# A hybrid encoder layer on one core: weight loads moved to another queue, diagonal copies moved to the VectorE, and the 32x32 products of an inverse spread over four array tiles

## The chip, the core and the metric

The kernel runs on one core of a Trainium2 chip. The engines are written as in the profile: PE is the matrix engine (TensorE), PEld its weight loads, DVE the VectorE, ACT the ScalarE, POOL the GpSimd, SP the SyncE, which here only issues DMAs. The metric is the device time of one execution in microseconds (us); lower is better.

## The reference, cut to what matters

One encoder layer on 1024 tokens of width 1024, float32. One input projection feeds three branches: windowed attention, a bidirectional RWKV-7 scan, and sigmoid gates. The branches are lifted, gated, summed and projected; two more residual blocks (a feed-forward one and a small gated one) follow.

```python
def rwkv7_bidir_scan(r, w, k, v, a, b):
    def step(state, inp):
        r_t, w_t, k_t, v_t, a_t, b_t = inp
        sa = jnp.einsum('dbhij,dbhj->dbhi', state, a_t)
        state = (state * w_t[..., None, :] + sa[..., :, None] * b_t[..., None, :]
                 + v_t[..., :, None] * k_t[..., None, :])
        y = jnp.einsum('dbhij,dbhj->dbhi', state, r_t)
        return state, y
...
        h = rms_norm(x, norm_mix[i])
        proj = h @ w_in[i]
        attn = windowed_gqa(q, k, v, sink[i])
        rw = rwkv7_time_mix(zr, w0[i], w2[i], a0[i], a2[i], g2[i], k_k[i], k_a[i],
                            r_k[i], lnx_w[i], lnx_b[i])
        gates = jax.nn.sigmoid(proj[..., O_GATE:].reshape(bsz, s, N_BRANCH, D_MODEL))
        merged = gates[..., 0, :] * (attn @ w_up_attn[i]) + gates[..., 1, :] * (rw @ w_up_rwkv[i])
        x = x + merged @ w_out[i]
        hf = rms_norm(x, norm_ffn[i])
        x = x + jnp.square(jax.nn.relu(hf @ w_ff1[i])) @ w_ff2[i]
        hp = rms_norm(x, norm_ple[i])
        x = x + (p[i] @ w_ple[i]) * jax.nn.sigmoid(hp @ w_ple_gate[i])
```

The kernel computes the scan in 16 chunks of 64 tokens. Each chunk needs, for each of 8 heads and 2 directions, the inverse of a 64x64 triangular matrix; it is built from two 32x32 inverses on its diagonal and one product of three 32x32 matrices off it.

## The kernel before, in words

Dense products are made with three matmuls each: an operand is split into a high and a low part (`split`: a copy on ACT, then a subtraction on DVE or POOL), and `mm3_steps` yields after each of high x high, low x high, high x low. A group of such matmuls is a "step" of a filler, and the fillers are what keeps PE busy while the scan and the attention wait for other engines.

In order of time:

- 0 to about 280 us: normalisation, projections of the RWKV columns in four pairs of heads, with decay and in-context rates. For each pair, `vt` is eight transposes of z (`vtp`, L633), copied by ACT and stored to `v_d` (L635); `bv` (L636 to L640) is a bonus term that uses PE sums `px` (L619, L620) and is stored to `bv_d`. Both `vt` and `bv` take the buffer with tag "vt", which has one copy.
- 280 to about 480 us: the attention, in 8 blocks of 128 queries (loop over `n`, from L914): scores `sc` (L934), softmax on DVE and ACT, transposes `pt` (L955), products `po` (L963), a store `at_d`. Steps of `gates(0)` (matmuls `gmm`; weights by `load_w`, staged in `wst` L215, loaded on SP's queue, split into `whi`, `wlo`) stand between them. Inside this loop the triangular matrices of scan block 0 are made too: `low_products` (matmuls `lps` L813 from `la`, `lb`, copied to `lt` L815, four chunk pairs), then `inverse` (copies `Lc`, transpose `Lp`, a recurrence of 31 steps `tmp`/`Z` on DVE, transposes `Zn`, `Zt`).
- 480 to about 770 us: the scan, in four blocks of four chunks. At the start of each block, `inverse_off` makes the 32x32 products: 64 products `qps<-Zn,lt`, copies `Q` (L861), steps of the filler (`between()`, 8 of them), 64 products `qps<-Zt,Q` and `qps<-Q,Zt`, and copies into `zi`. Each product is one matmul in the code and two records in the trace, so a group shows as 128. The inverse of the next block is prepared meanwhile: `low` (one chunk pair of `lps`, ACT's copies `lt` and `Lc` L1279), and `inverse_steps` (the recurrence, from `Lp` L1285). The filler is `beside()`: the rest of the gates, then the lift of the attention branch (`uaps`, from weights `wuhi`/`wulo`, the attention output `aTh`/`aTl`, and a gate read back from `g_d`).
- 770 to about 800 us: `epilogue(1)`, group normalisation of the scan's second half: sums `mups`, logarithms `lv` and exponentials `ysq` on ACT.
- 800 us to the end: the lift of the scan branch (`mmc`, gated in `g1t`, split into `mh`/`ml`), the output projection `mmo` with weights `wo0h`/`wo0l`, the feed-forward part (`ff1ps`, `ff2ps`) and the last gate.

Each engine runs its instructions in a fixed order that a scheduler makes from the code, with priorities; `after(a, b)` puts instruction a behind b in it. PE's array can be used in tiles of 32 rows by 32 columns; a matmul whose operands lie on partitions 32r to 32r+31 and whose output lies on partitions 32c to 32c+31 uses row group r and column group c.

Of the kernel before, what the change touches and what calls it, by code (L numbers as in the profile page):

```python
# [17 lines left out]
P = 128  # L18
# [19 lines left out]
EXPIN = (1, 0)  # L38
# [17 lines left out]
GATT = 1  # L56

# [10 lines left out]
LOW_AT = 3  # L68
# [77 lines left out]
def block_kernel(ctx: ExitStack, tc: tile.TileContext, I: dict, out: bass.AP):  # L146
# [49 lines left out]
    def split(hi, lo, src, lo_eng=None, pin=False):  # L196

        a = nc.scalar.copy(hi, src)  # L198
        b = (lo_eng or nc.vector).tensor_tensor(out=lo, in0=src, in1=hi.bitcast(F32), op=ALU.subtract)  # L199
        if lo_eng is nc.gpsimd:  # L200
            on_pool[0] = b
        if pin:
            tc.keep_in_program_order(a)
            tc.keep_in_program_order(b)

    def load_w(pl, tag, src, n, bufs=2, sbufs=2, lo_eng=None, stag=None, parts=1, stages=()):
# [5 lines left out]
        for i in range(0, k, step):  # L212
            spl, stg, sb = stages[(i // step) % len(stages)] if stages else (pl, stag or tag + "_st", sbufs)
            st = spl.tile([P, step, n], F32, name="wst", tag=stg, bufs=sb)
            nc.sync.dma_start(st, src[:, i:i + step])  # L215
# [105 lines left out]
    def gates(h, ms=range(2 * KT), mm=nc.tensor.matmul, lo_of=lambda m: nc.gpsimd):  # L321

        for m in ms:
            c0 = O_GATE + m * P
            hi, lo = load_w(PW, "w", w_col(c0), P, parts=2, lo_eng=lo_of(m))
# [191 lines left out]
    with ExitStack() as s1:  # L517
# [106 lines left out]
        def add_bonus(p, rk, vz):  # L624
# [11 lines left out]
            bv = A1.tile([P, T], F32, name="bv", tag="vt", bufs=1)  # L636
# [213 lines left out]
    def inverse_off(pl, ps_of, lt, zz, zi, mm, between):  # L850
# [5 lines left out]
        for i in range(32):  # L856
            for r in (0, 2):
                mm(qss[i // 16][g[r + 1], i % 16, :], lt[g[r], i, 32:64], Zn[g[r], i, :], start=True, stop=True)
        for hp, qs in enumerate(qss):
            for r in (1, 3):  # L860
                nc.scalar.copy(Q[g[r], 16 * hp:16 * hp + 16, :], qs[g[r]])  # L861
# [7 lines left out]
        for i in range(32):  # L869
            mm(qss[i // 16][g[0], i % 16, :], Q[g[1], i, :], Zt[g[1], i, :], start=True, stop=True)  # L870
            mm(qss[i // 16][g[3], i % 16, :], Zt[g[3], i, :], Q[g[3], i, :], start=True, stop=True)
        for hp, qs in enumerate(qss):
            nc.scalar.copy(zi[g[0], 16 * hp:16 * hp + 16, 32:64], qs[g[0]])
            nc.scalar.copy(zi[g[3], 16 * hp:16 * hp + 16, 0:32], qs[g[3]])
# [26 lines left out]
    with ExitStack() as s2:  # L901
# [16 lines left out]
        for n in range(NT):  # L918
# [53 lines left out]
            if n == LOW_AT:  # L972
                lts[0] = list(low0)[-1]
# [18 lines left out]
    def beside():  # L992
# [18 lines left out]

        def weights(m, st=None):
            hi = UA.tile([P, NP, P], F32R, name="wuhi", tag="wu_hi", bufs=3)
            lo = UA.tile([P, NP, P], F32R, name="wulo", tag="wu_lo", bufs=3)
            split(hi, lo, st or load_wu(UA, m))
# [12 lines left out]
        for h in range(2):  # L1028
            hs = slice(512 * h, 512 * h + 512)
            for m in range(KT):  # L1030
                hi, lo = ahead.pop(0)
                if (h, m) != (0, 0) and (h, m) < (1, KT - 1):
                    ahead.append(weights((m + 1) % KT))
                g = UA.tile([P, 512], F32, name="gta", tag="g1t", bufs=2)
                nc.sync.dma_start(g, g_d[m, :, hs])
# [27 lines left out]
    def epilogue(e):  # L1063
# [50 lines left out]
        for p in range(NP):  # L1114
# [12 lines left out]
            split(rwh[:, p, :], rwl[:, p, :], rs.rearrange("q a t -> q (a t)"))  # L1127
# [873 lines left out]
```

## Time and profile before

| what | value |
|---|---|
| three runs, median | 1685.11 us (1683.96, 1685.11, 1685.51) |
| profiled execution | 1685.89 us |
| its span, first to last instruction | 1684.1 us |
| around the span | 1.79 us |
| PE busy | 1615.9 us, 96% |
| PEld / DVE / ACT / POOL busy | 1307.8 / 1134.6 / 844.5 / 103.1 us |
| mean granted TensorE clock | 0.986 |
| DMA | 269.23 MB, mean 160 GB/s |

PE is busy for 96% of the span, so the time is PE's work plus the 68.2 us in which PE has nothing to run, plus what PE loses where its granted clock is below 1. The clock is granted in stretches; a slower stretch shows in the windows of the profile as a mean below 1. A row of the view of waits names the engine that waited, the line and tile it waited to start, and what ended the wait.

### The profile page before, as it was taken

The page shows a single profiled execution, that of the slowest core. Times are in us where ns is not written, and L with a number is a line of the kernel's source. Part 1 is how long each engine was busy: PE and PEld are TensorE (multiplying, and loading weights), DVE is VectorE, ACT ScalarE, POOL GpSimd, SP SyncE. Part 2 cuts the span into 40 slices and gives each one's busy share as a digit, 9 for nine tenths or more (in the row PEclk, how much of TensorE's full clock was granted, in tenths as well). Part 3 has the DMA queues.
Part 4 walks back from the last instruction along what each step waited for, and adds up shares of the span by engine and source line. Part 5 has one row for each costly group of instructions (what it writes and reads, how often), then busy time and mean ns, then how long its engine had stood idle before and what let it go on. Part 6 is the DMA issues. An engine that isn't in the chain of part 4 may idle for free.

```text
span 1684.1 us, 31165 instructions
## 1 busy us (share of the span) xinstructions
PE 1615.9 (96%) x12280; PEld 1307.8 (78%) x12280; DVE 1134.6 (67%) x2055; ACT 844.5 (50%) x1535; POOL 103.1 (6%) x113
## 2 busy tenths in 40 slices
PE   7999998899999999898999999999999999999998
PEld 7987776776677787676778788888888888888887
DVE  5648998265947596777744876667667877685342
ACT  5557887367744545456313554444435344544121
POOL 3440000221200000000000000000000000000000
PEclk9999999999999999799999999999999999999999
DMA  6353556764286554547652154444449865564110
GB/s 223 82 155 98 171 163 202 227 172 130 88 230 198 139 179 134 163 130 238 207 179 100 57 177 161 144 165 147 138 167 349 273 204 162 164 212 148 38 41 38
DMA packets 200834, 269.23 MB, mean 160 GB/s; under 512 B 47728, under 2 KB 103920, under 8 KB 200688
## 3 DMA queue, kind: packets, MB, share of 16 engines
q1 hardware_dynamic: 190752, 254.14, 47.6%
q0 software_dynamic: 9792, 12.59, 2.9%
q8 instruction: 96, 1.57, 0.4%
q10 hardware_dynamic: 144, 0.52, 0.1%
q14 instruction: 50, 0.41, 0.1%
HBM read 186.45 MB, written 80.74 MB: 159 GB/s over the span
## 4 chain that ended last, share of the span: by engine, by line
PE 74%; DVE 10%; DMA 6%; ACT 5%; issue 3%; POOL 1%; SPq 0%; DVEq 0%; ACTq 0%; POOLq 0%
PE ff2ps L1882 18%; PE ff1ps L1630 16%; PE gmm L221 4%; DMA wst<-in_w_col_dram 2%; PE plps L231 2%; PE plps L229 2%; PE plps L227 2%; PE mm L239 2%; PE mm L240 2%; PE mm L241 2%; PE uaps L221 1%; PE gps L221 1%; PE mmo L241 1%; PE mmo L239 1%; PE mmo L240 1%
## 5 line engine op out<-in xcount | busy, mean ns | idle before, releaser
L1882 PE MATMUL ff2ps<-th,sl 128*128 128x512 f32 x448 | 174.3, 389 | 0.0
L1882 PE MATMUL ff2ps<-tl,sh 128*128 128x512 f32 x448 | 174.3, 389 | 0.0
L1882 PE MATMUL ff2ps<-th,sh 128*128 128x512 f32 x448 | 173.9, 389 | 0.0
L198 ACT CAST sh<-sst 128x512 fp32r<-128x512 f32 x109 | 67.8, 622 | 100.4 <-PE ff2ps L1882 50.9
L199 DVE TENSOR_TENSOR sl<-sst,sh 128x512 fp32r<-128x512 f32 x109 | 75.0, 688 | 44.0 <-ACT sh L198 43.5
L1630 PE MATMUL ff1ps<-mh,w1h 128*128 128x512 f32 x256 | 100.3, 392 | 2.0 <-ACT w1h L198 2.0
L198 ACT CAST whi<-wst 128x512 fp32r<-128x512 f32 x100 | 60.3, 618 | 81.9 <-DMA wst<-in_w_col_dram 30.3
L1630 PE MATMUL ff1ps<-ml,w1h 128*128 128x512 f32 x256 | 99.9, 390 | 0.0
L1630 PE MATMUL ff1ps<-mh,w1l 128*128 128x512 f32 x256 | 99.6, 390 | 0.0
L1882 PEld LDWEIGHTS ff2ps<-tl,sh 128*128 128x128 f32 x448 | 84.1, 188 | 17.7 <-DVE tl L199 0.2
L1882 PEld LDWEIGHTS ff2ps<-th,sh 128*128 128x128 f32 x448 | 84.0, 188 | 17.6 <-ACT th L198 0.3
L1882 PEld LDWEIGHTS ff2ps<-th,sl 128*128 128x128 f32 x448 | 84.1, 188 | 17.5
L183 POOL TENSOR_TENSOR rstd<-ms,neghalf 128x1 f32<-128x1 f32 x24 | 14.5, 606 | 1019.7 <-PE ff2ps L1882 572.3
L198 ACT CAST w1h<-w1st 128x512 fp32r<-128x512 f32 x48 | 28.3, 620 | 96.3 <-DMA w1st<-in_w_ff_dram 59.6
L199 DVE TENSOR_TENSOR wlo<-wst,whi 128x512 fp32r<-128x512 f32 x72 | 47.9, 687 | 29.5 <-ACT whi L198 29.4
L199 DVE TENSOR_TENSOR w1l<-w1st,w1h 128x512 fp32r<-128x512 f32 x48 | 31.7, 687 | 51.6 <-ACT w1h L198 51.6
L227 PE MATMUL gmm<-hh,whi 128*128 128x512 f32 x136 | 57.0, 419 | 4.6 <-ACT whi L198 4.6
L1630 PEld LDWEIGHTS ff1ps<-mh,w1h 128*128 128x128 f32 x256 | 48.1, 188 | 12.9 <-ACT w1h L198 2.8
L231 PE MATMUL gmm<-hh,wlo 128*128 128x512 f32 x136 | 56.8, 419 | 0.0
L1630 PEld LDWEIGHTS ff1ps<-mh,w1l 128*128 128x128 f32 x256 | 48.1, 188 | 10.9 <-DVE w1l L199 0.8
L229 PE MATMUL gmm<-hl,whi 128*128 128x512 f32 x136 | 56.5, 416 | 0.0
L1630 PEld LDWEIGHTS ff1ps<-ml,w1h 128*128 128x128 f32 x256 | 48.1, 188 | 10.0
(405 smaller groups left out, 4530.9 us busy)
## 6 DMA issues: line engine op xcount, KB each, us to landing
wst<-in_w_col_dram SPq DMA_DIRECT2D x92, 256.0 KB, 3.4
tst<-in_w_ff_dram SPq DMA_DIRECT2D x80, 256.0 KB, 4.1
w1st<-in_w_ff_dram SPq DMA_DIRECT2D x32, 512.0 KB, 5.1
hid_S<-h SPq DMA_DIRECT2D x64, 256.0 KB, 2.1
sst<-hid_S SPq DMA_DIRECT2D x64, 256.0 KB, 3.2
hid_A<-h SPq DMA_DIRECT2D x48, 256.0 KB, 2.0
sst<-hid_A SPq DMA_DIRECT2D x45, 256.0 KB, 4.0
ra_d<-ra SPq DMA_DIRECT2D x8, 1024.0 KB, 5.7
```

The lines of the kernel that those rows point to most:

```text
L183: nc.gpsimd.tensor_tensor(out=r, in0=ms, in1=neghalf.broadcast_to([P, width]), op=ALU.pow)
L198: a = nc.scalar.copy(hi, src)
L199: b = (lo_eng or nc.vector).tensor_tensor(out=lo, in0=src, in1=hi.bitcast(F32), op=ALU.subtract)
L221: tc.keep_in_program_order(nc.tensor.matmul(*a, **kw))
L227: mm(ps, ah, bh, start=(i == 0), stop=False)
L229: mm(ps, ah, bl, start=False, stop=False)
L231: mm(ps, al, bh, start=False, stop=(i == n - 1))
L239: nc.tensor.matmul(ps, ah, bh, start=(i == 0), stop=False)
L240: nc.tensor.matmul(ps, ah, bl, start=False, stop=False)
L241: nc.tensor.matmul(ps, al, bh, start=False, stop=(i == n - 1))
L1630: nc.tensor.matmul(ps, x_[:, k, :], y_[:, k, :], start=start and k + i == 0, stop=k == 3 and i == 2, skip_group_check=True)
L1882: nc.tensor.matmul(banks[bs][i], x_[:, isl], y_, start=fresh and p + j == 0, stop=p == NPR - 1 and j == 2, skip_group_check=True)
```

## The change

It has seven parts.

1. `GQ`: the gate weights of m=1 and m=2 of `gates(0)` (four loads `wst` of 256 KB) go out on POOL's queue and no longer on SP's.
2. The last pair's `bv` takes the buffer with tag "kd" instead of "vt".
3. `LOW_AT = (3, 4)`: of scan block 0's `low_products`, two chunk pairs are made in attention block 3 and two in block 4 (before: all four in block 3).
4. The diagonal copies `Lc` of scan blocks 1 to 3 (48 of 32x256) are made by DVE and no longer by ACT, each after the next chunk pair's products, the last ahead of `Lp`.
5. `inverse_off`: products with even and odd index go to two different column groups, so that four array tiles are used (before: two). In the first group, row 0's products go to columns 1 and 3 and row 2's to columns 3 and 1 (before: 0 to 1, 2 to 3), and each row group has a PSUM tile of its own (before: each half of the indices). The copies read every second index's place, from a partition group that is not the one they write for half of them.
6. `beside()`: the third up-weight and the first gate tile `gta` are requested before the first `wuhi` split, and the gate's load is `gate_of`.
7. `EXPIN = (1, 1)`: in `epilogue(1)` the exponentials come after the last logarithm, as in `epilogue(0)` already; and the splits of `wo0` are put behind the epilogue's last split.

```diff
-EXPIN = (1, 0)
+EXPIN = (1, 1)
+GQ = ((0, 1), (0, 2))
-LOW_AT = 3
+LOW_AT = (3, 4)
...
-            nc.sync.dma_start(st, src[:, i:i + step])
+            (q or nc.sync).dma_start(st, src[:, i:i + step])
...
-            hi, lo = load_w(PW, "w", w_col(c0), P, parts=2, lo_eng=lo_of(m))
+            hi, lo = load_w(PW, "w", w_col(c0), P, parts=2, lo_eng=lo_of(m), q=nc.gpsimd if (h, m) in GQ else None)
...
-            bv = A1.tile([P, T], F32, name="bv", tag="vt", bufs=1)
+            bv = A1.tile([P, T], F32, name="bv", tag="kd" if p == NP - 1 else "vt", bufs=1)
...
         for i in range(32):
             for r in (0, 2):
-                mm(qss[i // 16][g[r + 1], i % 16, :], lt[g[r], i, 32:64], Zn[g[r], i, :], start=True, stop=True)
-        for hp, qs in enumerate(qss):
-            for r in (1, 3):
-                nc.scalar.copy(Q[g[r], 16 * hp:16 * hp + 16, :], qs[g[r]])
+                c = (r + 1 + 2 * (i % 2)) % 4
+                mm(qss[r // 2][g[c], i // 2, :], lt[g[r], i, 32:64], Zn[g[r], i, :], start=True, stop=True)
+        for r in (0, 2):
+            for k in range(2):
+                nc.scalar.copy(Q[g[r + 1], k::2, :], qss[r // 2][g[(r + 1 + 2 * k) % 4]])
...
-            mm(qss[i // 16][g[0], i % 16, :], Q[g[1], i, :], Zt[g[1], i, :], start=True, stop=True)
-            mm(qss[i // 16][g[3], i % 16, :], Zt[g[3], i, :], Q[g[3], i, :], start=True, stop=True)
-        for hp, qs in enumerate(qss):
-            nc.scalar.copy(zi[g[0], 16 * hp:16 * hp + 16, 32:64], qs[g[0]])
-            nc.scalar.copy(zi[g[3], 16 * hp:16 * hp + 16, 0:32], qs[g[3]])
+            k = i % 2
+            mm(qss[0][g[2 * k], i // 2, :], Q[g[1], i, :], Zt[g[1], i, :], start=True, stop=True)
+            mm(qss[1][g[3 - 2 * k], i // 2, :], Zt[g[3], i, :], Q[g[3], i, :], start=True, stop=True)
+        for k in range(2):
+            nc.scalar.copy(zi[g[0], k::2, 32:64], qss[0][g[2 * k]])
+            nc.scalar.copy(zi[g[3], k::2, 0:32], qss[1][g[3 - 2 * k]])
...
-            if n == LOW_AT:
-                lts[0] = list(low0)[-1]
+            if n in LOW_AT:
+                for _ in range(NB // len(LOW_AT)):
+                    lts[0] = next(low0)
...
+        sts.append(load_wu(UA, 2))
+        gta = [gate_of(0, 0)]
...
-                    ahead.append(weights((m + 1) % KT))
-                g = UA.tile([P, 512], F32, name="gta", tag="g1t", bufs=2)
-                nc.sync.dma_start(g, g_d[m, :, hs])
+                    ahead.append(weights((m + 1) % KT, sts.pop(2) if sts[2:] else None))
+                g = gta.pop() if gta else gate_of(m, h)
...
-            split(rwh[:, p, :], rwl[:, p, :], rs.rearrange("q a t -> q (a t)"))
+            epi["done"] = split(rwh[:, p, :], rwl[:, p, :], rs.rearrange("q a t -> q (a t)"))
...
     def low(b, ci):
-        lt = lts[b] = next(lows[b])
-        if ci == 0:
+        if ci:
+            diagonal(b, ci - 1)
+        else:
             Lcs[b] = BI.tile([P, 32, 32], F32, name="Lc", tag="inv", bufs=3)
+        lts[b] = next(lows[b])
+    def diagonal(b, ci):
+        lt = lts[b]
         for r0 in range(0, P, 32):
             k = r0 // 32 % 2
-            nc.scalar.copy(Lcs[b][r0:r0 + 32, 8 * ci:8 * ci + 8], lt[r0:r0 + 32, 8 * ci:8 * ci + 8, 32 * k:32 * k + 32])
+            turn(nc.vector.tensor_copy(Lcs[b][r0:r0 + 32, 8 * ci:8 * ci + 8], lt[r0:r0 + 32, 8 * ci:8 * ci + 8, 32 * k:32 * k + 32]))
     def inverse_steps(b):
+        diagonal(b, NB - 1)
...
-            split(wo[n][0][:, k:k + 2], wo[n][1][:, k:k + 2], st)
+            split(wo[n][0][:, k:k + 2], wo[n][1][:, k:k + 2], st, behind=None if n else epi["done"])
```

How the change moves instructions is shown at three places, by the order of the program's instructions on one engine; a row has its number, the line (line numbers of the changed kernel are 4 to 22 higher), the operation, output<-input, the output's shape and, where equal rows follow one another, their count.

POOL's queue at about 280 us. `qT` and `kT` are the attention's queries and keys, `wlo` POOL's share of the splits. Before:

```order
46 L401 DMA qT_d<-qkT 128x512 x2
47 L403 DMA kT_d<-qkT 512x1x128
48 L754 DMA qT<-qT_d 128x1024
49 L767 DMA qT<-qT_d 128x1024
50 L762 DMA kT<-kT_d 128x4x256
51 L199 TENSOR_TENSOR wlo<-wst,whi 128x512 x2
```

With the change:

```order
47 L407 DMA kT_d<-qkT 512x1x128
48 L219 DMA wst<-in_w_col_dram 128x512 x2
49 L758 DMA qT<-qT_d 128x1024
50 L219 DMA wst<-in_w_col_dram 128x512
51 L771 DMA qT<-qT_d 128x1024
52 L219 DMA wst<-in_w_col_dram 128x512
53 L766 DMA kT<-kT_d 128x4x256
54 L200 TENSOR_TENSOR wlo<-wst,whi 128x512 x2
```

Two of the four weight loads now stand ahead of the first `qT`, the third and fourth ahead of the second `qT` and the first `kT`; on SP's queue the four are gone from behind the stores of `bk`, `v`, `ra` and `bv`.

PE just ahead of the attention's first scores, at about 331 us. Before, 20 gate matmuls follow `px` before the first `sc`; the first of them are:

```order
1336 L633 MATMUL vtp<-ident,z 128x128
1337 L619 MATMUL px<-s_1410,one_r 128x512
1338 L620 MATMUL px<-s_1410,one_r 128x512
1339 L619 MATMUL px<-s2h,one_r 128x512
1340 L620 MATMUL px<-s2l,one_r 128x512
1341 L229 MATMUL gmm<-hl_93,whi 128x512
1342 L231 MATMUL gmm<-hh_92,wlo 128x512
```

With the change:

```order
1334 L637 MATMUL vtp<-ident,z 128x128 x8
1335 L623 MATMUL px<-s_1410,one_r 128x512
1336 L624 MATMUL px<-s_1410,one_r 128x512
1337 L623 MATMUL px<-s2h,one_r 128x512
1338 L624 MATMUL px<-s2l,one_r 128x512
1339 L233 MATMUL gmm<-hl_93,whi 128x512
1340 L235 MATMUL gmm<-hh_92,wlo 128x512
1341 L231 MATMUL gmm<-hh_92,whi 128x512
1342 L233 MATMUL gmm<-hl_93,whi 128x512
1343 L235 MATMUL gmm<-hh_92,wlo 128x512
1344 L940 MATMUL sc<-kT,qT 128x256 x4
```

The eight transposes `vtp`, of which seven stood among gate matmuls some 40 us earlier, are now together ahead of `px`, and the scores follow five gate matmuls after `px`.

ACT in scan block 0, after the first group of 32x32 products, about 482 to 510 us (`tm`, `W`, `UV`, `y` are the scan's own copies). Before:

```order
405 L874 COPY zi<-qps 32x16x32
406 L815 COPY lt<-lps 128x4x64 x2
407 L1279 COPY Lc<-lt 32x256 x4
408 L198 CAST whi<-wst 128x512 x2
409 L1237 COPY UV<-ups 64x512 x2
410 L1216 COPY W<-wa 128x512
411 L329 ACTIVATE gth<-gmm 128x512
412 L198 CAST whi<-wst 128x512
413 L815 COPY lt<-lps 128x4x64 x2
414 L198 CAST whi<-wst 128x512
415 L1279 COPY Lc<-lt 32x256 x4
```

With the change:

```order
414 L880 COPY zi<-qps 32x16x32
415 L819 COPY lt<-lps 128x4x64 x2
416 L1252 COPY UV<-ups 64x512 x2
417 L1231 COPY W<-wa 128x512
418 L199 CAST whi<-wst 128x512
419 L333 ACTIVATE gth<-gmm 128x512
420 L199 CAST whi<-wst 128x512
421 L819 COPY lt<-lps 128x4x64 x2
422 L1280 COPY y<-wy_4972 128x2x2x64
423 L1280 COPY y<-wy_4973 128x2x2x64
424 L819 COPY lt<-lps 128x4x64 x4
```

The `Lc` copies are gone from ACT; on DVE four of them stand between two `gm` products and twelve in a row directly ahead of `Lp`.

More of the change, by code (lines that the diff above doesn't have):

```diff
@@ L194, in block_kernel, with split @@
     on_pool = [None]
-    def split(hi, lo, src, lo_eng=None, pin=False):
+    def split(hi, lo, src, lo_eng=None, pin=False, behind=None):
         a = nc.scalar.copy(hi, src)
         b = (lo_eng or nc.vector).tensor_tensor(out=lo, in0=src, in1=hi.bitcast(F32), op=ALU.subtract)
+        for x_, y_ in zip((a, b), behind or ()):
+            after(x_, y_)
         if lo_eng is nc.gpsimd:
@@ L204, in split, with load_w @@
             tc.keep_in_program_order(b)
-    def load_w(pl, tag, src, n, bufs=2, sbufs=2, lo_eng=None, stag=None, parts=1, stages=()):
+        return a, b
+    def load_w(pl, tag, src, n, bufs=2, sbufs=2, lo_eng=None, stag=None, parts=1, stages=(), q=None):
         k = src.shape[1]
@@ L971, in block_kernel @@
                 zi = zi_tile(BI, "zi")
-            if n == LOW_AT:
-                lts[0] = list(low0)[-1]
+            if n in LOW_AT:
+                for _ in range(NB // len(LOW_AT)):
+                    lts[0] = next(low0)
+            if n == LOW_AT[-1]:
                 for d in range(ND):
@@ L1010, in beside, with gate_of @@
         aTl = UA.tile([P, NP, 512], F32R, name="aTl", tag="aTl", bufs=1)
+        def gate_of(m, h):
+            g = UA.tile([P, 512], F32, name="gta", tag="g1t", bufs=2)
+            nc.sync.dma_start(g, g_d[m, :, 512 * h:512 * h + 512])
+            return g
+        sts.append(load_wu(UA, 2))
+        gta = [gate_of(0, 0)]
         def weights(m, st=None):
@@ L1014, in weights @@
             lo = UA.tile([P, NP, P], F32R, name="wulo", tag="wu_lo", bufs=3)
-            split(hi, lo, st or load_wu(UA, m))
+            split(hi, lo, load_wu(UA, m) if st is None else st)
             return hi, lo
```

## The prediction, made before the changed kernel ran

> **What bounds the kernel now.** I read the page's busy times first, then the view of waits of PE, then the granted clock in windows, and last the places of the change in the timeline.
>
> ```profile
> PE 1615.9 (96%) x12280; PEld 1307.8 (78%) x12280; DVE 1134.6 (67%) x2055; ACT 844.5 (50%) x1535; POOL 103.1 (6%) x113
> ```
>
> PE is busy 96% of the span. The time falls only where PE waits less, runs at full clock longer, or has less to do. The waits (us in total, times, longest):
>
> ```profile
> PE gmm L227 <- ACT whi L198: 4.6, 1, 4.6
> PE qps L221 <- DVE Zn L1300: 4.3, 1, 4.3
> PE sc L934 <- DVE bv L638: 4.3, 1, 4.3
> PE pt L955 <- DVE smk L952: 4.1, 3, 2.0
> PE mups L221 <- ACT rwh L198: 3.8, 3, 2.4
> PE uaps L221 <- ACT aTh L198: 3.7, 1, 3.7
> PE wy L221 <- issue: 3.5, 2, 2.2
> PE lps L221 <- ACT lt L815: 3.1, 2, 1.7
> PE lps L813 <- DMA lb<-bk_d: 2.5, 1, 2.5
> PE mups L221 <- DVE rwl L199: 1.6, 4, 0.6
> PE tmps L1185 <- ACT lt L815: 1.4, 2, 0.7
> ```
>
> The windows show what follows such waits. Columns: stretch, length, busy time of PE, PEld, DVE, ACT, POOL with counts, clock, DMA share, GB/s.
>
> ```profile
> 280.00:300.00 20.00, 15.39 (x60) 11.62 (x58) 13.91 (x14) 9.15 (x13) 1.49 (x3) 0.83 0.96 290
> 335.00:350.00 15.00, 13.60 (x62) 11.18 (x63) 6.26 (x28) 5.26 (x18) 6.02 (x6) 0.89 0.68 208
> 350.00:480.00 130.00, 119.53 (x767) 82.48 (x766) 98.17 (x309) 90.91 (x241) 21.91 (x21) 0.97 0.47 136
> 500.00:570.00 70.00, 64.24 (x1455) 53.10 (x1455) 50.97 (x112) 34.14 (x71) 1.11 (x2) 0.95 0.61 177
> 680.00:700.00 20.00, 16.04 (x291) 12.54 (x289) 14.69 (x38) 8.46 (x16) 0.00 (x0) 0.83 0.68 206
> 700.00:725.00 25.00, 20.66 (x528) 17.23 (x528) 17.79 (x31) 10.43 (x19) 0.00 (x0) 0.80 0.44 142
> 1000.00:1250.00 250.00, 250.00 (x1097) 205.71 (x1096) 172.41 (x275) 113.61 (x198) 0.00 (x0) 1.00 0.45 152
> ```
>
> The clock is below 1 only in stretches that hold a long wait. Length times (1 - clock) is the PE time lost: 3.4, 1.65, 3.9, 3.5, 3.4 and 5.0 us in the first six rows. So a wait costs itself and often half as much again. From 1000 us on PE is full (250.00 of 250.00, one 128x512 matmul per 0.228 us); the change touches nothing there.
>
> **The change, part by part.** Gains are positive.
>
> *1, gate weights on POOL's queue.*
>
> ```profile
> 280.44 4.16 SPq L640 DMA_DIRECT2D bv_d<-bv  x2
> 284.69 1.09 SPq L215 DMA_DIRECT2D wst<-in_w_col_dram  x2
> 278.67 0.62 ACT L198 CAST whi<-wst 128x512 fp32r<-128x512 f32 x1 [1.40 <-PE mm L229]
> 293.47 0.62 ACT L198 CAST whi<-wst 128x512 fp32r<-128x512 f32 x1 [4.66 <-DMA wst<-in_w_col_dram]
> 279.62 0.56 POOL L754 DMA_DIRECT2D qT<-qT_d  x1 [162.43 <-PE px L221]
> qT<-qT_d POOLq DMA_DIRECT2D x2, 512.0 KB, 9.1
> ```
>
> The previous use of the staging buffers ended with the cast at 278.67, but SP stood at `bv_d`'s stores and issued the loads only at 284.69; they landed 8.8 us later. POOL was idle, so it can issue about 5.4 us sooner. This removes at most the wait 4.6 and the slow clock 3.4, 8.0. Even if the loads take the 9.1 us of `qT` on the same queue, they land near 288.4, 5 us sooner than now. The queue's cost: `qT` and `kT` go out behind the loads, some 2 us later each; the scores that need them start at 336. The DMA share of 0.96 stays, so I take 6; range 2 to 8. A sentence apart: the Trainium skill, SBUF — State Buffer, Who interferes with whom, says that a DMA issued from GpSimd's queue is starved of descriptors while DVE holds the shared port; by it the loads would wait for DVE's casts and the gain would be near its lower end. No row here separates that from the busy DMA engines.
>
> *2, `bv` in another buffer.*
>
> ```profile
> 331.02 0.43 SPq L635 DMA_DIRECT2D v_d<-vt  x1
> 335.65 1.29 DVE L638 TENSOR_TENSOR bv<-px,z 128x512 f32<-128x512 f32 x2 [22.38 <-DMA v_d<-vt]
> ```
>
> `bv` waits for the store of the `vt` that shares its buffer, and the scores wait for `bv`. With another buffer it starts when `px` ends. The five gate matmuls left between cover 1.14 us of its 1.29. Gone: 4.3 + 1.65 less a rest; I take 5 (3 to 6). The fifteen matmuls that stood there move behind, and are PE's work either way.
>
> *3, low products in two blocks.*
>
> ```profile
> 466.94 1.99 DVE L844 STREAM_TRANSPOSE Zt<-Z 128x1024 f32<-128x1024 f32 x1
> 481.29 2.21 PE L221 MATMUL qps<-Zn,lt 32*32 32x32 f32 x128
> ```
>
> The wait on `lb`, 2.5, goes: its loads are issued a block ahead of use. Half of the 3.9 us of clock belongs to it (the other to `pt`'s 2.0). 4.4 at most; at least 0, if the second half is late in its new place. I take 3.5. The recurrence begins one block later; it ended at 468.9, 12 us ahead of the first `qps`, which covers that.
>
> *4, diagonal copies on DVE.*
>
> ```profile
> L1279 ACT COPY Lc<-lt 32x256 f32<-32x256 f32 x48 | 19.3, 403 | 0.8
> L864 DVE COPY zi<-Zn 32x1024 f32<-32x1024 f32 x8 | 5.5, 687 | 0.2
> 689.56 0.69 DVE L199 TENSOR_TENSOR wulo<-wust,wuhi 128x512 fp32r<-128x512 f32 x1 [4.14 <-ACT wuhi L198]
> ```
>
> ACT loses 19.3 us, and its `lt` copies come sooner: 3.1 of `lps`, 1.4 of `tmps`, and half of the 3.5 us of clock, 6.2 in all. I take 5 (2 to 6.2). DVE gains 48 copies of between 0.17 (a quarter of 687) and 0.40 us, 2.7 to 6.4 us in each scan block, where it is busy 51 of 70. Twelve stand ahead of `Lp`, so the recurrence starts later; in block 3 the 4.14 us that DVE idles ahead of `wulo` cover it, 1.3 once part 6 has taken its 2.85.
>
> *5, four array tiles.*
>
> ```profile
> 704.64 3.62 PE L221 MATMUL qps<-Zn,lt 32*32 32x32 f32 x128 [4.30 <-DVE Zn L1300]
> 566.89 0.80 PE L221 MATMUL wy<-Sc,rac 64*64 64x64 f32 x19 [2.22 <-issue]
> L861 ACT COPY Q<-qps x16: 577/578/582, 482.5 to 708.9; 32x512 f32<-32x512 f32 x16
> ```
>
> A group of 128 records takes 2.21 us (481.29), 34 ns per record and tile, and 3.62 at the slow clock, so the array and not the issue sets it. If four tiles run beside each other, 1.1 is left: 8 x 1.1 = 8.8. But the row with "issue" comes right behind a group: PE had run out of instructions, and a faster group only reaches that point sooner. Against it, too: the four `Q` copies (2.31 us) can start only when the whole group is done, where two started half way; eight filler matmuls cover 8 x 0.228 = 1.8. That costs about 0.5 in each of three blocks. I take a third of the bound, 3; range -2 to 8.8. Copies that cross partition groups stand nowhere in this trace; I price them like the 0.578 they replace; twice that would be part of the low end.
>
> *6, earlier requests for the lift.*
>
> ```profile
> 688.91 0.62 ACT L198 CAST wuhi<-wust 128x512 fp32r<-128x512 f32 x1 [2.85 <-DMA g_d<-gth]
> 702.44 2.05 DVE L1300 STREAM_TRANSPOSE Zn<-Z 128x1024 f32<-128x1024 f32 x1
> ```
>
> `wuhi` waits 2.85 us for the store of the last gate. In the new order it waits only for its own load. What it releases is a chain on DVE (`wulo`, `aTl`, the recurrence's last steps, `Zn`) on which PE waits next, 4.3. So the whole 2.85 is won there, and no clock beyond it: `Zn` stays late. 2.85 (0 to 3.7).
>
> *7, epilogue.*
>
> ```profile
> L1103 ACT ACT_TABLE_LOAD x3 | 3.8, 1283 | 0.1
> L199 DVE TENSOR_TENSOR wo0l<-wst,wo0h 128x1024 fp32r<-128x1024 f32 x4 | 4.9, 1220 | 0.5 <-ACT wo0h L198 0.5
> 792.51 0.50 PE L221 MATMUL mups<-rwh,one_r 128*128 128x512 f32 x1 [2.38 <-ACT rwh L198]
> ```
>
> Two table loads (2.57) and four casts leave ACT's path to `mups`; of its 5.4 us of waits I take 3.3. Two `wo0l` (2.44) then stand ahead of the first gated product on DVE, for which `mmc` and `mmo` wait: back go 2.3. Net 1 (-1.5 to 3.3).
>
> **The sum.** 6 + 5 + 3.5 + 5 + 3 + 2.85 + 1 = 26.35; the low ends give 3.5, the high ends 40.4. Orders moved this much make a new wait somewhere; I charge one like `lb`'s with its clock, 4.4. The profiled execution took 1685.89, 0.8 above the median: 1685.89 - 26.35 + 4.4 = 1663.9, and 1663 beside the median.
>
> **The rivals.**
>
> *The products double their speed and no wait takes the place of those gone*: +5.8 on part 5 and no 4.4, 1653. For it: 3.62 against 2.21 says that the array binds. Against: the "issue" row. In sentences apart: the Trainium skill, TensorE: Matmul & The Clock Gate, Part 3, has tiles start about 4 ns apart, which would bear this out; but it also says that a weight load overlaps a running matmul only if the row group differs, and the new tiles differ in columns alone.
>
> *The products gain nothing*, since a row group's loads and matmuls follow one another whatever the column: part 5 is -1.5 instead of 3, 1668. For it: two tiles in two row groups are all the concurrency that the rows show. This is the change not doing what it says; the page's second rule stands for it.
>
> *The stalls are only handed on*: the loads of part 1 land late in a DMA stretch at 0.96, the new `lps` place waits, and `Zn` takes what part 6 gives. Parts 1, 3 and 6 at their low ends: 1663 + 4 + 3.5 + 2.85 = 1673.
>
> *No change*: the low ends and the new wait nearly cancel, 1685.
>
> *Slower, by instruction supply*: each faster group runs PE dry, 2.2 us as in the "issue" row plus 3.4 us of slow clock, 5.6 for each of eight. It ends above 1688.5 once five of the eight do so (5 x 5.6 = 28 against the 25.5 between 1663 and 1688.5). Against: one of eight does now, and the supply that a group uses stays the same.
>
> **How the numbers follow.** Chances: forecast 0.42, doubled 0.17, no gain of the products 0.17, handed on 0.14, no change 0.05, slower 0.05. Faster by over 0.2% (3.4 us, about what can be told from no change here) is 0.90. Leaving out a tenth on each side: from 1651, below the doubled case, to 1679, above the handed-on one.
>
> **What would show it.** After the change the rows of `gmm<-whi`, `sc<-bv`, `lps<-lb` and `lps<-lt` should be gone or under 1 us, and the clock of 280:300 and 335:350 at 1. A `qps` group should last under 2.2 us; if 1.1, the doubled case. `uaps` should wait about 1 us and `qps<-Zn` still some 4. I am wrong if POOL's loads land after 290, if `issue` waits exceed 6 us, or if new waits above 2 us stand in the attention.

## The result: faster, by two fifths of the forecast

| what | before | changed |
|---|---|---|
| median of the runs compared | 1685.31 us (1683.96 to 1687.87) | 1676.72 us (1672.79 to 1678.14) |
| profiled execution, its span | 1685.89, 1684.1 | 1677.99, 1676.2 |
| mean granted clock | 0.986 | 0.984 |

The ratio is 0.9947, with a 95% interval of 0.9932 to 0.9961. The gain is 8.6 us where 22 were forecast: the direction and the range hold, the size does not. Runs of one kernel here spread over up to 17 us, and a profile is of one of them; so below, medians and ratios tell what an edit is worth, and a profile tells where one execution waited.

The engines and the waits of PE in the changed kernel, from its page and its view of waits (us in total, times, longest):

```profile
PE 1609.2 (96%) x12280; PEld 1302.1 (78%) x12280; DVE 1156.5 (69%) x2103; ACT 820.7 (49%) x1485; POOL 104.8 (6%) x117
...
PE tmps L1200 <- DVE gm L1183: 8.9, 2, 8.6
PE qps L225 <- DVE Zn L1322: 5.1, 1, 5.1
PE pt L961 <- DVE smk L958: 5.0, 6, 1.4
PE wy L225 <- issue: 4.8, 2, 2.4
PE gmm L231 <- ACT whi L199: 2.4, 1, 2.4
...
PE mups L225 <- ACT rwh L199: 1.5, 3, 0.6
...
PE uaps L225 <- ACT aTh L199: 0.8, 1, 0.8
...
PE sc L940 <- ACT vt L638: 0.4, 1, 0.4
```

Nearly every wait that the change was aimed at is gone or small: `lps` on `lt` and on `lb` have no row left, `sc` waits 0.4 instead of 4.3, `uaps` 0.8 instead of 3.7, the longest `mups` 0.6 instead of 2.4. Behind a wait at the program's start that both kernels have (`tp<-xs`, 9.7 and 10.6), a wait that the kernel before did not have stands first: `tmps<-gm`, 8.6 us in one piece. The windows (columns as in the prediction):

```profile
280.00:300.00 20.00, 19.38 (x83) 14.50 (x82) 13.94 (x16) 10.54 (x15) 3.50 (x6) 1.00 0.99 306
300.00:320.00 20.00, 17.04 (x65) 12.76 (x64) 8.91 (x11) 7.34 (x13) 4.00 (x4) 0.91 0.75 218
335.00:350.00 15.00, 13.13 (x71) 9.90 (x69) 10.25 (x41) 10.05 (x35) 5.35 (x6) 1.00 0.72 226
470.00:500.00 30.00, 20.09 (x420) 15.35 (x420) 7.18 (x13) 9.82 (x17) 1.11 (x2) 0.73 0.70 220
455.00:478.00 23.00, 15.23 (x121) 11.76 (x120) 12.38 (x16) 3.96 (x7) 2.54 (x2) 0.91 0.98 273
```

280:300 and 335:350 are at full clock as foretold, and then a stretch of 30 us from 470 holds 20.09 us of PE work at a clock of 0.73. The kernel before had there:

```profile
470.00:500.00 30.00, 28.59 (x614) 22.08 (x612) 8.97 (x17) 11.06 (x22) 1.11 (x2) 1.00 0.90 248
```

From the records of both profiles I counted, stage by stage, the time in which no matmul ran, and half of the matmul time at a clock of 0.5 as time lost to the clock. What is left of a span, less its start and tail without matmuls, is called work.

| stage (us) | before: idle + clock | changed: idle + clock |
|---|---|---|
| 0 to 280 | 3.9 + 0 | 4.3 + 1.7 |
| 280 to 470 (attention) | 18.1 + 7.9 | 12.5 + 1.7 |
| 470 to 500 (first scan block) | 1.4 + 0 | 9.9 + 5.5 |
| 500 to 680 | 8.9 + 4.7 | 6.7 + 6.1 |
| 680 to 725 (last scan block) | 8.3 + 6.9 | 7.8 + 5.3 |
| 725 to 860 | 11.0 + 0 | 9.4 + 0 |
| 860 to the end | 2.5 + 0 | 2.3 + 0 |
| work | 1596.4 | 1589.0 |

The attention won 11.8 us and the first scan block lost 14.0. Over the whole span idle and clock stay at 73.5 and 73.3; in this pair of profiles nearly all that was won is 7.4 us of work.

**The place.** The last `po` of the attention and the `tmps` that follow in the scan, in the timeline (start, length); the kernel before:

```profile
465.62 2.62 PE L963 MATMUL po<-pT,V 128*64 128x512 f32 x8
479.39 1.03 PE L1185 MATMUL tmps<-ident,bkc 128*128 128x128 f32 x8
457.90 1.71 SPq L215 DMA_DIRECT2D wst<-in_w_col_dram  x2
```

The changed kernel, with SP's queue, ACT and DVE between them:

```profile
452.15 1.94 PE L969 MATMUL po<-pT,V 128*64 128x512 f32 x8
457.50 0.86 SPq L904 DMA_DIRECT2D bkc<-bk_d  x2
468.13 1.99 SPq L1003 DMA_DIRECT2D gm<-at_d  x4
470.17 0.91 SPq L1007 DMA_DIRECT2D wust<-in_w_up_attn_dram  x2
471.17 0.85 SPq L219 DMA_DIRECT2D wst<-in_w_col_dram  x2
476.99 0.62 ACT L199 CAST whi<-wst 128x512 fp32r<-128x512 f32 x1 [10.03 <-DMA wst<-in_w_col_dram]
467.14 1.02 DVE L1183 TENSOR_TENSOR gm<-gps,gmask 128x384 f32<-128x384 f32 x2 [0.79 <-PE gps L225]
477.64 0.69 DVE L200 TENSOR_TENSOR wlo<-wst,whi 128x512 fp32r<-128x512 f32 x1 [9.47 <-ACT whi L199]
478.25 1.01 DVE L1183 TENSOR_TENSOR gm<-gps,gmask 128x384 f32<-128x384 f32 x2
478.85 1.97 PE L1200 MATMUL tmps<-ident,bkc 128*128 128x128 f32 x8 [8.62 <-DVE gm L1183]
```

PE ends the attention 14.2 us sooner (452.15 + 1.94 against 465.62 + 2.62), but reaches `tmps` 0.5 us sooner. Two of the four `gm` (scan masks) are made at 467.14. The other two stand, in DVE's fixed order, behind the `wlo` of a gate weight for the second half of the tokens (m=1; a weight comes in two loads, and this is its second). That load is requested at 471.17: SP first issues the scan's operands from 457.50 on, the attention output's reload (`gm<-at_d`, another tile of the same name) and two up-weights. It is cast at 476.99, 5.8 us after its request, with the DMA engines busy 0.98 of 455 to 478. In the kernel before both loads of this weight went out from 457.90 on, the second at 459.29, ahead of the reload and the operands. So in the changed kernel DVE idles 9.47 us and PE 8.62, and the clock stays low behind it.

### The profile page after: what moved, and what is told of

Read it like the earlier page. It is cut to its first block, busy times and chain, and to the rows that moved or that the text cites. A ratio compares the mean times of both kernels' runs of the same rounds, so it can differ in the third digit from the quotient of the medians.

```text
span 1676.2 us, 31183 instructions
## 1 busy us (share of the span) xinstructions
PE 1609.2 (96%) x12280; PEld 1302.1 (78%) x12280; DVE 1156.5 (69%) x2103; ACT 820.7 (49%) x1485; POOL 104.8 (6%) x117
## 4 chain that ended last, share of the span: by engine, by line
PE 69%; DVE 14%; DMA 7%; ACT 4%; issue 3%; SPq 1%; POOL 1%; DVEq 0%; POOLq 0%; ACTq 0%
PE ff2ps L1904 18%; PE ff1ps L1652 16%; DMA wst<-in_w_col_dram 3%; PE gmm L225 2%; PE plps L235 2%; PE plps L233 2%; PE plps L231 2%; PE mm L243 2%; PE mm L244 2%; PE mm L245 2%; DVE tmp L1315 1%; DVE Z L1318 1%; DMA g1t<-g_d 1%; PE mmo L245 1%; PE mmo L244 1%
## 5 line engine op out<-in xcount | busy, mean ns | idle before, releaser
L200 DVE TENSOR_TENSOR sl<-sst,sh 128x512 fp32r<-128x512 f32 x109 | 75.0, 688 | 48.3 <-ACT sh L199 48.0
```

## The experiments

Each run has its own runs of the kernel before beside it, on the same chip; ratios are to those. First, *the changed kernel itself, run again* beside the last two of the experiments:

> The changed kernel itself, unchanged, on the same chip as the next two, so that they are compared without the difference between chips. Its long wait at tmps (8.0 to 10.2 us in every kernel so far that keeps its order there) is in the kernel's order and not in one execution: 7 us or more again, 1674 to 1679, 0.4 to 0.7% below the kernel before.

Measured: 1678.21 us (1671.07 to 1681.73), ratio 0.9957 [0.9941, 0.9973], as expected. The longest `tmps<-gm` is again 8.6.

**The four array tiles.** *The changed kernel with the old `inverse_off`*:

```diff
-                mm(qss[r // 2][g[c], i // 2, :], lt[g[r], i, 32:64], Zn[g[r], i, :], ...)
+                mm(qss[i // 16][g[r + 1], i % 16, :], lt[g[r], i, 32:64], Zn[g[r], i, :], ...)
```

> The changed kernel with part 5 undone: the 32x32 products on two array tiles as before, everything else changed. Theory A (the new 8.62 us wait before tmps, with its slow clock some 15 us, ate the gain; the products are worth little): the same long wait stays at about 470 to 479 us, and the time is 1676 to 1681, within 4 us of the changed kernel's 1676.7. Rival B (the four tiles cost: their copies and the drier instruction supply took the gain): 1662 to 1670. Rival C (the four tiles bring the full 8.8 us): 1684 to 1687.

Measured: 1677.04 us, ratio 0.9962 [0.9946, 0.9979], as theory A says, and the longest `tmps<-gm` is still 8.2; the interval overlaps the changed kernel's, so the products are worth nothing that can be measured there. *The kernel before with the new `inverse_off`* (the same lines the other way round):

> The kernel before with part 5 alone. Theory A: the groups last 1.3 to 2.2 us where they took 2.21, the two waits with the releaser issue grow by about as much; 1682 to 1685. Rival B (it costs): above 1687. Rival C (full gain): 1676 to 1679.

Measured: 1685.2 us, ratio 1.0021 [1.0010, 1.0033]: no gain, but a small loss, 0.2 us above theory A's range. Yet the groups are faster. At the half clock the first group of scan block 0 takes 3.62 us with the old products (first row, of that run) and 1.93 with the new (second, of the changed kernel):

```profile
483.31 3.62 PE L225 MATMUL qps<-Zn,lt 32*32 32x32 f32 x128
```

```profile
482.46 1.93 PE L225 MATMUL qps<-Zn,lt 32*32 32x32 f32 x128
```

By the count above, the new products take 4.8 us of work away from the kernel before (1596.4 to 1591.6), and putting the old ones back adds 7.6 to the changed one (1589.0 to 1596.6). In the run with the products alone, idle rises by the same 4.8 (54.0 to 58.8). Its waits of PE show where a part of it went:

```profile
PE wy L221 <- issue: 5.2, 2, 2.8
PE qps L221 <- ACT Q L862: 1.1, 2, 0.6
PE gmm L221 <- issue: 1.0, 1, 1.0
```

`issue` (the profile shows nothing that PE waited for; the prediction reads it as a lack of instructions) was 3.5 at `wy` and is 6.2 in these rows, and the second groups now wait for the last of the `Q` copies.

**The low part that holds `gm`.** *Only that one `wlo` moves from DVE to POOL*:

```diff
-        yield from gates(1, range(GATT, 2 * KT), mmo, lo_of=lambda m: nc.vector)
+        yield from gates(1, range(GATT, 2 * KT), mmo, lo_of=lambda m: nc.gpsimd if m == 1 else nc.vector)
```

> The changed kernel, but for the gate weight m=1 of the second half the subtraction wlo runs on POOL and not on DVE. No load moves: SyncE's queue keeps its order, so this weight lands as late as before. Theory A (DVE's fixed order is what holds: wlo waits for the late weight and the gm products that PE needs stand behind it): the 8.62 us wait at tmps falls below 2 and the clock stays at 1 there; 1661 to 1666. Rival D (the late load itself holds PE: the gate matmuls that need it come next in PE's order): the wait moves to gmm with 5 us or more; 1672 to 1677.

Measured: 1672.49 us, ratio 0.9941 [0.9927, 0.9954]. The 8.62 is gone and `tmps` starts at 469.04, 9.8 us sooner than in the changed kernel, as theory A says; but the time is above its range, and the interval overlaps the changed kernel's. The timeline of PE shows what is late next:

```profile
474.68 0.21 PE L225 MATMUL qps<-Zn,lt 32*32 32x32 f32 x1 [2.48 <-issue]
476.82 0.80 PE L225 MATMUL gmm<-hh,whi 128*128 128x512 f32 x1 [1.94 <-ACT whi L199]
492.37 0.55 PE L225 MATMUL gps<-rac,bkc 64*64 64x128 f32 x2 [3.71 <-ACT zi L879]
```

The matmuls with the late weight itself wait 1.94; around them PE runs dry once and waits for a copy of `zi` once: 8.1 us in three pieces for the 8.6 in one.

*The two late weights go out on POOL's queue*: `GQ` gets (1, 1) and (1, 2) too.

> The changed kernel, but the gate weights m=1 and m=2 of the second half are loaded from POOL's queue too, so that they no longer stand behind the scan's operands and the attention output on SyncE's queue. Theory A: they land before 470 us, the 8.62 us wait and its slow clock go, 1661 to 1666, as with the subtraction moved. Rival E (the DMA engines are full from 457 to 475, so that queue order does not help): the weights land at 475 or later all the same, wait 5 us or more, 1672 to 1677.

Measured: 1673.12 us, ratio 0.9947 [0.9932, 0.9961]. Its waits of PE:

```profile
PE qps L225 <- DVE Zn L1322: 7.8, 1, 7.8
PE gps L225 <- DVE gm L1183: 6.6, 3, 6.1
```

The held load's cast now starts at 465.68, 11.3 us sooner than in the changed kernel, so the place in the queue did matter, and rival E's reason falls. But the four casts are spread from 461 to 473, and in DVE's order all four `wlo` now stand ahead of the `gm`: the masks for `gps` are held instead, 6.1 us.

*The attention output's reload and the up-weights are requested three gate weights later* (the two lines move down):

```diff
-        load_at(0)
-        sts = [load_wu(B, m) for m in range(2)]
-        yield from gates(1, range(GATT, 2 * KT), mmo, lo_of=lambda m: nc.vector)
+        yield from gates(1, range(GATT, 4), mmo, lo_of=lambda m: nc.vector)
+        load_at(0)
+        sts = [load_wu(B, m) for m in range(2)]
+        yield from gates(1, range(4, 2 * KT), mmo, lo_of=lambda m: nc.vector)
```

> The changed kernel, but the loads for the attention's lift (1 MB of attention output, 0.5 MB of weights, needed some 200 us later) are requested three gate weights later, out of the stretch behind the attention. Theory F: 1.5 of 6.3 MB leave a stretch that moves 270 GB/s, 5.5 us of transfer; the late weight lands 3 to 6 us earlier and the wait at tmps falls from 8.6 to 3 to 6; 1669 to 1674. Rival G (it is the order on the queue of the other operands alone): the wait stays above 7, 1675 to 1678.

Measured: 1673.77 us, ratio 0.9938 [0.9923, 0.9952], as theory F says; `tmps<-gm` is 3.2 instead of 8.6, and `issue` ahead of `gps` 2.8 is new. *The same with (1, 1) on POOL's queue*:

> As the kernel with the attention's output requested later, and the gate weight m=1 of the second half on POOL's queue as well. Theory F: both the volume and the order are relieved; the waits from 465 to 500 us, 9 us or more in each of the three kernels so far, fall below 4, the clock there stays at 1; 1662 to 1668. Rival H (PE has too few gate matmuls between the attention and the scan, whatever lands when): 1669 to 1674, a wait of 4 us or more for gm or for operands remains.

Measured: 1673.6 us, ratio 0.9938 [0.9921, 0.9956], rival H's time, though no wait of 4 us stands there: at the first `qps` PE now leads the kernel before by 12.4 us. It loses part of that in the last scan block:

```profile
PE qps L225 <- DVE Zn L1323: 8.3, 1, 8.3
```

**Parts 1 to 3.** *`LOW_AT = (3,)`: part 3 undone alone.*

> The changed kernel with part 3 undone: all four chunk pairs of the low products in attention block 3. My estimate for part 3 was 3.5. If it holds, the wait on lb (2.5) with its slow clock comes back in the attention, and the end of the attention is some 4 us later. Theory F: that is not seen in the end, 1673 to 1678. Rival: part 3 is what makes the weight late, by the order that it gives to the loads; then the 8.6 us wait at tmps is gone and the time is 1664 to 1671.

Measured: 1672.47 us, ratio 0.9936 [0.9917, 0.9955], between the two ranges and not slower than with part 3. The long wait at the first `tmps` is gone, as the rival says; the wait on `lb` is back with 1.4, and the attention ends 2.0 us later. The four `gm` now stand ahead of the `wlo` in DVE's order (timeline of DVE and PE, the waits of PE below):

```profile
466.09 1.02 DVE L1183 TENSOR_TENSOR gm<-gps,gmask 128x384 f32<-128x384 f32 x2 [4.51 <-PE gps L225]
468.04 1.02 DVE L1183 TENSOR_TENSOR gm<-gps,gmask 128x384 f32<-128x384 f32 x2 [0.93 <-PE gps L225]
480.18 1.28 DVE L200 TENSOR_TENSOR wlo<-wst,whi 128x512 fp32r<-128x512 f32 x2
470.91 1.29 PE L225 MATMUL qps<-Zn,lt 32*32 32x32 f32 x128
683.43 0.69 DVE L200 TENSOR_TENSOR wulo<-wust,wuhi 128x512 fp32r<-128x512 f32 x1 [3.61 <-ACT wuhi L199]
...
PE qps L225 <- DVE Zn L1322: 8.5, 1, 8.5
```

The weight is no sooner (cast at 477.11), but it holds nothing up: `qps` starts at 470.91, 11.5 us sooner. At the `tmps` ahead of the last block the lead on the kernel before is 19.7 us. There the fourth `wulo` waits 3.61 us for a late up-weight and stands ahead of the last recurrence steps and `Zn`, and PE waits 8.5: the same pattern a second time, and at the block's `qps` 15.4 us of lead are left.

*Parts 1, 2 and 3 undone together* (`GQ = ()`, `bv` in "vt", `LOW_AT = (3,)`):

> The changed kernel with parts 1, 2 and 3 undone (loads on SyncE's queue, bv in the old buffer, low products all in attention block 3); parts 4 to 7 stay. In the changed kernel's trace the attention ends 14.2 us earlier than before and the scan starts no earlier. Theory F (the transfers that the scan's first block needs fill the DMA engines from the attention's end on, so whatever the attention gains is waited for there): the attention ends some 14 us later than in the changed kernel, the 8.62 us wait at tmps is gone, and the time is 1674 to 1680, within 4 us of the changed kernel. Rival G (only the order of the weight load is at fault, and the attention's gain is otherwise real): 1681 or more, that is the parts 4 to 7 alone.

Measured: 1680.72 us, ratio 0.9983 [0.9970, 0.9996], between the two ranges; parts 4 to 7 alone are worth about 2.9 us (0.7 to 5.1). Its waits of PE, in a profile of its slowest execution (1687.09):

```profile
PE qps L225 <- DVE Zn L1322: 8.8, 1, 8.8
...
PE gmm L231 <- ACT whi L199: 4.6, 2, 4.2
PE sc L940 <- DVE bv L642: 4.3, 1, 4.3
```

The two waits of parts 1 and 2 are back, 4.2 and 4.3, the first `tmps` does not wait for `gm`, and `Zn` has grown from the 4.3 of the kernel before to 8.8.

**Part 4 and the last block.** *The diagonal copies back on ACT*, the rest as changed:

> The changed kernel with part 4 undone: ScalarE makes the 48 diagonal copies again. My estimate for part 4 was 5: by it the waits lps<-lt and tmps<-lt come back (4.5 us and a stretch of slow clock), 1680 to 1683. Theory I (in the last block DVE's chain from Lp to Zn sets the end of the block, and the twelve copies ahead of Lp lengthen it by 3.6 us): the waits come back in blocks 0 to 2, but Lp of the last block starts 2 to 4 us earlier against the block's start and qps<-Zn waits 1 to 2.5 instead of 5.1; 1676 to 1680.

Measured: 1679.56 us, ratio 0.9980 [0.9967, 0.9994]: part 4 is worth some 3.9 to 5.6 us (0.9957 and 0.9947 against 0.9980, times 1685; the interval of the first, to 0.9973, just overlaps). The time is in theory I's range, but not for its reason: `Zn` waits 5.9. The waits on `lt` are not back by name; `tmps<-gm` grows to 10.2 instead. *On ACT in block 3 alone* (`if b == 3: nc.scalar.copy(...)`) asks whether the wait for `Zn` comes from the start of its chain, where the twelve copies stand, or from its end, the late `wulo`:

> The changed kernel, but the diagonal copies of the last block alone go to ScalarE. Theory I: what part 4 won in blocks 0 and 1 stays, Lp of the last block starts about 3 us earlier and the wait qps<-Zn falls from 5.1 to 2 to 3 us, its slow clock may go: 1671 to 1675. Rival J (DVE's chain is not paced by its start but by the scan's other work that stands in it, or ScalarE's lt copies wait instead): the wait stays within 1 us of 5.1, 1675 to 1678.

Measured: 1678.46 us, ratio 0.9973 [0.9962, 0.9985]; `Lp` starts 25.4 us after the block's first `qps` instead of 27.0, and the `Zn` wait stays at 5.2, so not from the start. *`LOW_AT = (3,)`, and every `wulo` but the first on POOL* tests the end:

```diff
-            split(hi, lo, load_wu(UA, m) if st is None else st)
+            split(hi, lo, load_wu(UA, m) if st is None else st, lo_eng=nc.gpsimd if m else None)
```

> The kernel with part 3 undone, in which qps<-Zn waited 8.45 us, and the low parts wulo of the lift's weights (but the first) made by POOL and not by DVE: three of 0.69 us fewer in DVE's chain of the last block, three fewer waits on wuhi in it. Theory I: Zn ends 2 to 5 us earlier, the wait falls to 3.5 to 6.5; 1666 to 1670. Rival J: the wait stays above 7.5, 1670 to 1674; or POOL's slower subtraction makes uaps wait instead.

Measured: 1672.61 us, ratio 0.9942 [0.9928, 0.9957]. Its waits of PE:

```profile
PE qps L225 <- DVE Zn L1322: 4.3, 1, 4.3
```

8.5 has become 4.3: DVE's idle ahead of the `wulo` between `Lp` and `Zn` fell from 6.7 us in three pieces to 1.5, and the stretch from 53.0 to 48.3. So the late up-weights were what lengthened the wait. But `Zn` ends no sooner, 689.5 against 689.1, since the recurrence starts 5.1 us later (`Lp` at 641.2 against 636.1): this execution had lost its lead before the last block. The time has not moved. *This edit and the one before it together*:

> As the run before, and the last block's diagonal copies on ScalarE as well: both reliefs of DVE's last chain on the kernel with part 3 undone. Theory I: together 5 to 8 us, the wait qps<-Zn falls below 3.5, its slow clock of 10 us shortens to 3.4 or nothing; 1662 to 1667, faster than the kernel before and than the changed one. Rival J: 1668 or more.

Measured: 1672.71 us, ratio 0.9947 [0.9927, 0.9966], rival J's; the `Zn` wait is 4.3 again.

In none of the 17 profiles is this wait below 4.2 us. One reason is DVE's own work, as this window of the changed kernel from `Lp` to the end of the last `Zn` shows (columns as above):

```profile
650.80:698.60 47.80, 40.57 (x871) 32.72 (x870) 44.57 (x113) 17.62 (x32) 0.00 (x0) 0.97 0.55 176
```

DVE has 44.6 us to do there and PE 40.6. In all 17 it is 44.5 to 46.7 and 40.5 to 42.9, so by an estimate from these figures some 4 us of the changed kernel's 5.1 stay however early the weights land.

**Is DVE's order all of it?** *All low parts of these weights on POOL* (the `wlo` of every gate weight from the attention's end on, and every `wulo` but the first):

> The changed kernel, but every subtraction of a weight's low part from the attention's end to the last scan block runs on POOL (30 wlo of the gates, the wulo of the lift but the first): no late load can hold DVE in its fixed order. No load moves. Theory K (the gain was lost by DVE being held behind late weights, at two places, the first tmps and the last Zn): neither place waits more than 3 us on DVE, 1664 to 1670, 5 us or more below the changed kernel. Rival D (the loads' lateness reaches PE another way, by ScalarE's casts or by gmm itself): waits of 5 us or more for ScalarE or for gmm in their place, 1671 to 1677.

Measured: 1678.08 us, ratio 0.9963 [0.9948, 0.9979], the same as the changed kernel run beside it and above both ranges. `tmps<-gm` is down to 1.2, and what waits now (among the waits of PE) is:

```profile
PE qps L225 <- DVE Zn L1322: 6.9, 3, 5.2
...
PE gps L225 <- ACT zi L879: 3.7, 2, 3.0
...
PE gmm L225 <- ACT whi L199: 2.9, 1, 2.9
```

This run did not only free DVE, it also slowed it. The timeline of POOL and DVE in it:

```profile
515.24 2.64 POOL L200 TENSOR_TENSOR wlo<-wst,whi 128x512 fp32r<-128x512 f32 x2 [11.52 <-ACT whi L199]
515.70 1.04 DVE L1315 TENSOR_TENSOR tmp<-Lp,Z 128x192 f32<-128x192 f32 x1
516.77 1.32 DVE L1318 TENSOR_TENSOR Z<-Z,tmp 128x192 f32<-128x192 f32 x1
```

The same two steps of the recurrence take 0.35 us each in the changed kernel, where POOL is idle beside them. In all 17 profiles no `tmp` or `Z` takes over 0.43 us unless it runs beside a subtraction on POOL; in this one, 20 of the 28 that do take 0.96 to 1.42. So DVE's busy time from the last `Lp` to the end of `Zn` rose from 44.6 to 46.7 us, though subtractions had left it.

*The same with the later requests and `LOW_AT = (3,)`*:

> As the run before, with the attention's output requested three gate weights later and the low products in one attention block, the two edits that made the weights land earlier: both the lateness and the way it reaches PE are relieved. Theory K: the prediction's 1663 within 4 us, 1660 to 1667. Rival D: 1668 or more, with other waits of 3 us or more and slow clock behind them between 465 and 720 us.

Measured: 1682.9 us, ratio 0.9995 [0.9982, 1.0008]: all of the gain is lost. Its profile has `gmm<-gth` 4.9, `qps<-Zn` 7.0 and `lps<-lb` 2.5, and the same DVE time of 46.7 us. So taking the held instructions off DVE moved the stalls and won nothing; since it also made DVE slower, the two runs do not settle how much of the loss is DVE's order. No version tried is shown to beat the changed kernel: the best ratios, 0.9936 to 0.9942, overlap its two, 0.9947 and 0.9957.

## Why the prediction was right in direction and wrong in size

**The step that failed** is the last of the sum: "Orders moved this much make a new wait somewhere; I charge one like `lb`'s with its clock, 4.4". The parts were to win 26.35 and 8.6 came, so 17.8 us came back and not 4.4. In the traces the largest piece stands in the first scan block, where idle and slow clock grew by 14.0 us, more than three times the charge, with the 8.6 of `tmps<-gm` at its head. The prediction followed what the earlier parts release only as far as the end of the attention; behind it, a load that now went out 12 us later stood ahead of two `gm` in DVE's fixed order.

That wait is not all of the miss. By the ratios, parts 1 to 3 added 4.4 to 6.1 us to the rest (0.9957 and 0.9947 against 0.9983) where 14.5 were forecast, and parts 4 to 7 without them, where the first `tmps` does not wait, gave 2.9 where 11.85 were forecast: both halves fell short by about the same. And where the long wait was taken away, the time is not shown to be better, because other waits came in its place. So the error was to add up the gains of the parts with one small charge for all that they would release; where the larger part of the 17.8 goes is shown at one place, and why it does not come back when that place is relieved stays open. The nearest rival was "the stalls are only handed on", 1673: right in kind, though of the places it named (part 1's loads, `lps`, `Zn`) only the first and the last were partly right; the new wait stands at the first `tmps`.

**Parts 1 to 3** were to give 14.5 and gave 11.8 in the attention's stage. Part 2 is right (`sc` waits 0.4). Of part 1's 6, nearer 3 came (280 to 320 us: PE busy 36.4 instead of 35.4, clock 0.96 instead of 0.91). The wait of 4.6 and its slow stretch are gone, but the next weight, still on SP's queue, is late (`gmm<-whi`, 2.4), and the clock of 300:320 is 0.91, 1.8 us. From issue to the cast that waited for them, the three loads that POOL issued at 281.88, 283.32 and 291.07 took 7.5, 9.8 and 5.6 us, with the DMA engines 0.99 busy; the first, issued ahead of that stretch at 268.85, took 2.9. The two that SP issued in that stretch in the kernel before, at 284.69 and 285.36, took 8.8 and 9.3. So POOL's queue is not seen to cost anything here, and the effect on DMAs from GpSimd's queue that the prediction cites from the Trainium skill, SBUF — State Buffer, Who interferes with whom, does not show in this trace.

Part 3 was +3.5 and is at best nothing: `lb`'s wait went, but the new order placed the late `wlo` ahead of `gm`, and undoing it cost no time (0.9936).

**Part 4**: 5 forecast, 3.9 to 5.6 by the run without it. A copy took 284 ns on DVE, inside the bounds of 0.17 and 0.40:

```profile
L1300 DVE COPY Lc<-lt 32x256 f32<-32x256 f32 x48 | 13.7, 284 | 10.1 <-ACT lt L819 9.6
```

**Part 5** was 3 (-2 to 8.8). The 128 records take 1.29 us at full clock, not 2.21 and not quite 1.1. The work it saves, 4.8 to 7.6 us, lies between the 3 taken and the 8.8 of the "doubled" rival. The time it saves can't be told from nothing in the changed kernel, and is 0.2% the wrong way alone. So the doubled rival was right on the array and wrong on the time; "the products gain nothing" was right on the time for a reason it didn't have. The reason given against the gain, PE running dry sooner, agrees with the rows: `issue` on `wy` 3.5 to 4.8 (5.2 with the products alone, and 2.6 in the changed kernel with the old ones). The copies across partition groups cost what was assumed, 577 ns.

```profile
L866 ACT COPY Q<-qps x16: 574/577/582, 484.4 to 702.5; 32x512 f32<-32x512 f32 x16
```

The rule quoted in the prediction from the Trainium skill, TensorE: Matmul & The Clock Gate, Part 3, that a weight load overlaps a running matmul only if the row group differs, was no bar to the gain: with column tiles added within the same two row groups the group went from 2.21 to 1.29 us. But the change also gave each row group a PSUM tile of its own, where the two had shared one; no run separates the two, so whether the rule holds here stays open.

**Part 6** was 2.85, and `uaps` does wait 0.8 instead of 3.7; the stage of the last block won 2.1. As foretold, `Zn` stays late, 5.1, and in three runs the next up-weight makes it 8.3 to 8.8. **Part 7** was 1, and its stage won 1.6.

Of what was said to show the prediction wrong, one came in part: the last two of POOL's four loads landed after 290 (their casts waited for them until 293.17 and 296.63). `issue` stays under 6. Between the first scores and the scan no new wait is above 2; the 2.4 of `gmm<-whi`, at 309, stands ahead of the scores. The sign that mattered, a wait just behind the attention, was not on the list.

**What stays open.** In all 17 profiles counted in this way idle lies between 51.6 and 63.0 us, in all but one under 59, whatever stall an edit removed, while the clock's loss varies from 5.5 to 20.3. Which resource keeps it there was not settled: the DMA engines, 0.98 busy for 23 us behind the attention; DVE's chain from `Lp` to `Zn`, 41 to 53 us for a scan block of some 70; the casts on ACT; or whatever stands behind `issue`. The runs with all low parts on POOL do not settle it, since DVE ran slower in them. A run that moves those low parts to ACT, or that leaves DVE less to do between `Lp` and `Zn`, was not made.

## What to carry to other kernels

Before a stall's removal is counted as won, follow PE past it to the next thing that it does not make itself (here the next stage's operands, on a queue and on DMA engines that are already full), and count only the lead that is left there. In an engine with a fixed order, the cast or subtraction of a prefetched weight holds everything behind it whenever the load is late; look at what stands behind each such row, and at every load whose place in a queue the change moved. Before work is moved to another engine to relieve the first, look whether the first runs slower beside it. A matmul group that runs faster is worth its time only if what it waits for and the copies behind it keep up and no new idle follows: measure it alone. Gains of parts that meet in the same stretch don't add; measure them together and apart.

## What the runs showed of the hardware

- Four 32x32 tiles in two row groups and two column groups each ran 128 records in 1.29 us, two tiles in 2.21; at the half clock 1.93 and 3.62. Better by 1.7 to 1.9, not by 2. The four also wrote two PSUM tiles by row group, where the two shared one.
- ACT's copies from one partition group to another cost the same as straight ones, 577 against 578 ns.
- In bursts of small matmuls (most of them of 130 or more) PE idled for up to 2.8 us at a time with nothing in the profile to wait for (`issue`). In total it was 4.1 us with the old products (both kernels that have them), 4.8 to 5.3 in the two profiles of the changed kernel and 7.1 with the new products alone.
- A DVE operation on two inputs of the recurrence (`tmp`, `Z`: 0.19 to 0.43 us) took up to 1.49 us when it ran beside a POOL subtraction of 1.3 us.
- Slow stretches of the clock vary between runs of one kernel: in four runs of the changed kernel the mean clock ranged from 0.984 (1677.99 us) to 0.992 (1672.79 us). An edit worth a few us can't be read from one profile.
